# Gated layers as 2x2 block products with seven multiplications

## Chip, cores and metric

One core of a Trainium2 chip runs the whole program. The metric is the device time of one execution in microseconds, median of the runs shown.

## What is computed

Two transformer blocks over 512 tokens of 1024 features, in fp32, one sequence. The second block has two layers, and each of these has two gated layers with the attentions between them:

```python
def swiglu(h, w_gate, w_up, w_down):
    return (jax.nn.silu(h @ w_gate) * (h @ w_up)) @ w_down
...
    for l in range(DEPTH_2):
        x = x + 0.5 * swiglu(rmsnorm_2(x, ffn1_norm[l]), ffn1_w_gate[l], ffn1_w_up[l], ffn1_w_down[l])
        x = x + token_mixing(rmsnorm_2(x, mix_norm[l]), positions, w_in[l], ...)
        x = x + 0.5 * swiglu(rmsnorm_2(x, ffn2_norm[l]), ffn2_w_gate[l], ffn2_w_up[l], ffn2_w_down[l])
    return rmsnorm_2(x, final_norm)
```

The inner width D_FF is 2816, 22 tiles of 128 features.

## The kernel before

Activations lie with features on the 128 partitions and the 512 tokens along the free axis, so a matrix of 1024 features is eight row tiles of 128x512. TensorE works in its fast fp32 form, and to keep the accuracy each operand is split into a high part (ScalarE copies it into that form) and a low part (the rest, which VectorE or GpSimd subtracts). A product of two tiles is then three TensorE products: high by high, high by low, low by high (`mm3`, lines 227 to 229).

```python
    def split(self, hi, lo, src, pool=False):
        self.nc.scalar.activation(hi, src, AF.Copy)
        (self.nc.gpsimd if pool else self.nc.vector).tensor_tensor(lo, src, hi.bitcast(F32), op=ALU.subtract)
```

These are lines 202 and 203; most splits of the kernel are recorded under them. Weights come from HBM in units of 128x1024 (512 KB) through SyncE's queue into `wraw` and are split into `whi` and `wlo`; there are three buffers of each.

`ffn` is a gated layer; it runs four times (`which` 0 to 3). For each of the 22 inner tiles it loads a unit of gate and one of up, does 24 products of 512 columns for each into a PSUM bank, multiplies both by the norm's factor `rb` (lines 885 and 887, VectorE), takes silu (886, ScalarE), the product of the two (888, VectorE), and splits the result into `hid`. Since a norm's factor belongs to a token, that is, to a column, it can be applied behind the product: the operands `xs` are x times the gain, already split when x was finished, and `rb` itself is made by a chain of small steps (`norm`) whose TensorE pieces are put between the first products of the layer. Then come eight output tiles, each 66 products over all 22 tiles of `hid` (units of 8, 8 and 6 tiles). `residual` (line 852) adds half the result to x, and splits and squares it for the next norm (lines 206, 207, 324, 325). In the last gated layer the last output tile is done in two halves of the tokens, so that the final norm of one half lies beside the products of the other.

TensorE takes the instructions of the first two tiles of a layer in the order written; otherwise, in the gated layers, a planner with modelled durations orders each engine's instructions. Every engine then takes its own in that order. The attention (`mix`, lines 999 on) is written out in order for TensorE. Operands of layers lie in 28 slots of 4 KB for each partition, taken in turn.

## Time and profile before

| | us |
|---|---|
| median of 3 runs | 3024.08 |
| lowest and highest run | 3020.95, 3024.65 |
| span of the profiled execution | 3020.9 |
| granted TensorE clock in it, mean | 0.991 of 2.4 GHz |
| four gate/up stages | 253, 248, 248, 247 |
| four down stages | 123, 122, 122, 125 |
| two attention stages | 323, 324 |

The span runs from the first to the last instruction of the profiled execution. Stages are bounded by the first product of each kind, to a microsecond. What is left is the first block, 873 us, and the end.

### The profile page before, as it was taken

Reading aid. Unit: us, or ns where it says so; the run is one execution under the profiler, and the core shown is the slowest. Engines: PE = TensorE matmul, PEld = TensorE weight load, DVE = VectorE, ACT = ScalarE, POOL = GpSimd, SP = SyncE. Lnnn points to the kernel's source line nnn. Section 1 sums busy time; section 2 is a strip of 40 time slices with the busy share of each in tenths; the row PEclk is TensorE's granted clock in tenths of the full one; section 3 lists DMA queues with packets and bytes.
Section 4 is the critical chain, followed back from the end, with each engine's and each line's share of the span. In section 5 each row is a group of like instructions: output and inputs, shape, how many; then the busy total and the mean of one; then the engine's idle time right before and its main releaser. Section 6 shows DMA issues by size and latency. Waiting matters only on the chain.

```text
span 3020.9 us, 35009 instructions
## 1 busy us (share of the span) xinstructions
PE 2935.9 (97%) x13845; PEld 2387.9 (79%) x13845; DVE 1601.3 (53%) x2388; ACT 1272.8 (42%) x1917; POOL 417.8 (14%) x255
## 2 busy tenths in 40 slices
PE   6999999999999999989999999999999889999998
PEld 5888978888878888876788888888888767888887
DVE  7765665524455443488764443344433887644433
ACT  5665454423333222376743322223223767532322
POOL 4233430000000000243400000000002434100000
PEclk9999999999999999999999999999999999999999
DMA  6334332222223223211022223232322110122222
GB/s 233 111 123 140 137 135 82 92 97 94 95 92 100 92 94 96 89 56 43 29 70 93 96 89 96 94 98 91 96 89 94 57 49 29 63 91 98 92 95 73
DMA packets 79544, 278.06 MB, mean 92 GB/s; under 512 B 8811, under 2 KB 11115, under 8 KB 79380
## 3 DMA queue, kind: packets, MB, share of 16 engines
q1 hardware_dynamic: 79380, 275.82, 28.0%
q8 instruction: 109, 1.79, 0.2%
q14 instruction: 55, 0.45, 0.0%
HBM read 273.69 MB, written 2.10 MB: 91 GB/s over the span
## 4 chain that ended last, share of the span: by engine, by line
PE 89%; DVE 6%; issue 2%; ACT 1%; POOL 1%; DMA 0%; SPq 0%; POOLq 0%; DVEq 0%; ACTq 0%
PE up L227 5%; PE up L229 5%; PE up L228 5%; PE down L228 5%; PE gate L227 5%; PE down L229 5%; PE down L227 5%; PE gate L228 5%; PE gate L229 5%; PE ff L227 4%; PE ff L229 4%; PE ff L228 4%; PE pv L1320 2%; PE ptr L1302 2%; PE wo L229 1%
## 5 line engine op out<-in xcount | busy, mean ns | idle before, releaser
L202 ACT ACTIVATE whi<-wraw 128x1024 fp32r<-128x1024 f32 (+2 forms) x472 | 490.3, 1039 | 1286.9 <-issue 503.1
L203 DVE TENSOR_TENSOR wlo<-wraw,whi 128x1024 fp32r<-128x1024 f32 (+1 forms) x406 | 502.9, 1239 | 428.3 <-ACT whi L202 426.0
L203 POOL TENSOR_TENSOR wlo<-wraw,whi 128x1024 fp32r<-128x1024 f32 (+1 forms) x66 | 155.6, 2361 | 914.8 <-ACT whi L202 903.9
L228 PE MATMUL down<-hid,whi 128*128 128x512 f32 (+1 forms) x726 | 281.6, 388 | 0.0
L229 PE MATMUL down<-hid,wlo 128*128 128x512 f32 (+1 forms) x726 | 281.5, 388 | 0.0
L227 PE MATMUL down<-hid,whi 128*128 128x512 f32 (+1 forms) x726 | 280.9, 387 | 0.0
L887 DVE TENSOR_TENSOR u<-up,rb 128x512 f32<-128x512 f32 x88 | 60.8, 691 | 282.0 <-PE up L229 281.9
L227 PE MATMUL up<-xs,whi 128*128 128x512 f32 x528 | 209.4, 397 | 0.0
L227 PE MATMUL gate<-xs,whi 128*128 128x512 f32 x528 | 208.9, 396 | 0.0
L228 PE MATMUL up<-xs,whi 128*128 128x512 f32 x528 | 208.6, 395 | 0.0
L228 PE MATMUL gate<-xs,whi 128*128 128x512 f32 x528 | 208.5, 395 | 0.0
L229 PE MATMUL up<-xs,wlo 128*128 128x512 f32 x528 | 208.5, 395 | 0.0
L229 PE MATMUL gate<-xs,wlo 128*128 128x512 f32 x528 | 207.8, 394 | 0.0
L272 POOL TENSOR_TENSOR y<-ms,mhalf 128x4 f32<-128x4 f32 (+2 forms) x24 | 27.1, 1128 | 1293.2 <-DVE ms L271 1290.2
L885 DVE TENSOR_TENSOR t<-gate,rb 128x512 f32<-128x512 f32 x88 | 60.8, 691 | 197.5 <-PE gate L229 189.3
L228 PEld LDWEIGHTS down<-hid,whi 128*128 128x128 f32 x726 | 136.4, 188 | 30.7
L227 PEld LDWEIGHTS down<-hid,whi 128*128 128x128 f32 x726 | 136.3, 188 | 30.7
L229 PEld LDWEIGHTS down<-hid,wlo 128*128 128x128 f32 x726 | 136.5, 188 | 29.4
L227 PEld LDWEIGHTS up<-xs,whi 128*128 128x128 f32 x528 | 99.2, 188 | 24.2
L229 PEld LDWEIGHTS up<-xs,wlo 128*128 128x128 f32 x528 | 99.3, 188 | 23.8
L229 PEld LDWEIGHTS gate<-xs,wlo 128*128 128x128 f32 x528 | 99.2, 188 | 23.8
L227 PEld LDWEIGHTS gate<-xs,whi 128*128 128x128 f32 x528 | 99.2, 188 | 23.6
(562 smaller groups left out, 6844.0 us busy)
## 6 DMA issues: line engine op xcount, KB each, us to landing
wraw<-in_w2g SPq DMA_DIRECT2D x176, 512.0 KB, 3.5
wraw<-in_w2d SPq DMA_DIRECT2D x64, 512.0 KB, 3.5
ada<-in_ada SPq DMA_DIRECT2D x48, 512.0 KB, 5.3
wraw<-in_w1f SPq DMA_DIRECT2D x44, 512.0 KB, 3.5
wraw<-in_w1a SPq DMA_DIRECT2D x32, 512.0 KB, 3.4
wraw<-in_w1b SPq DMA_DIRECT2D x32, 512.0 KB, 3.4
wraw<-in_w2f SPq DMA_DIRECT2D x28, 512.0 KB, 3.5
wraw<-in_w2d SPq DMA_DIRECT2D x32, 384.0 KB, 3.0
```

Source lines behind the costliest of these rows:

```text
L202: self.nc.scalar.activation(hi, src, AF.Copy)
L203: (self.nc.gpsimd if pool else self.nc.vector).tensor_tensor(lo, src, hi.bitcast(F32), op=ALU.subtract)
L227: mm(out, ah, bh, start=start, stop=False)
L228: mm(out, ah, bl, start=False, stop=False)
L229: mm(out, al, bh, start=False, stop=stop)
L272: nc.gpsimd.tensor_tensor(y, ms, self.mhalf[:, :n], op=ALU.pow)
L885: nc.vector.tensor_tensor(t, og, rb, op=ALU.mult)
L887: nc.vector.tensor_tensor(u, ou, rb, op=ALU.mult)
L1302: nc.tensor.transpose(tr[:, b * P:(b + 1) * P], p[:, b * P:(b + 1) * P], self.c("ident"))
L1320: nc.tensor.matmul(o, values[b][:, h * P:(h + 1) * P], pt[i][:, b], start=b + i == 0, stop=b + i == NT)
```

## The change

A gated layer is cut into 2x2 blocks. For gate and up, the two rows of the weights' block matrix are gate (a11, a12) and up (a21, a22) of one inner tile, its columns the first and the last four of the eight row tiles of x; the other factor's blocks are these halves of x by the first and the last 256 tokens (b11, b12, b21, b22). For down, the rows are two neighbouring output tiles (n1 and n2), and the columns the two halves of a chunk of inner tiles. The 22 inner tiles make four chunks: three of 3 + 3 tiles, one of 2 + 2. A block product takes seven products of blocks where the plain way takes eight:

- sums of weights: s1 = a21 - a22, s3 = a21 - a11, s2 = a11 - s1, s4 = a12 - s2 (`g_block_weights`), each made on the chip and split like the three blocks that are used as they are;
- sums of the other factor: t1 = b12 - b11, t3 = b22 - b12, t2 = b22 - t1, t4 = b21 - t2 (`sums_of`), also made and split on the chip;
- seven products of 256 columns into three banks (`block`): into bank e one after the other a11 b11, s2 t2, s1 t1, s4 b22, into g s3 t3 and a22 t4, into f a12 b21. Between two of them the bank is read (`on`), so its running sums go to the right quarter of the result. The last product of a block is put off behind the second product of the next one.

The sums join tokens whose norm factors differ, so the factor cannot come in behind the products; the block operands of gate and up are made from x times gain times `rb` once the norm is there (`operands`); the first two inner tiles (0 and 3) stay plain products of `xs` (`Plain`, as before). A down product of a chunk begins when the first gate/up block of the next chunk is issued, and its seven results are added to x at once, each 256 columns (`Down.on`). After the last chunk `finished` does for two output tiles what `residual` did. The last unit of the last layer stays plain, in two halves of the tokens (`End`).

The six instructions marked `True` or `nc.gpsimd` in `g_block_weights` run on GpSimd, and in `operands` the sums of two of the four row pairs. Weights of an item are prepared one item ahead, one step after each product (`between`), and loaded two ahead. For the first gated layer the product of x with the earlier block's final norm moves from the chain of that norm into `operands`. TensorE now takes the instructions of a whole gated layer in the order written. `whi` and `wlo` of all stages come from one pool of ten buffers, `wraw` has four, the sums of weights two; slots go from 28 to 25. The last load of weights is now named for each load, so that loads stay in order. The host lays out up before gate, and the down weights by chunk (`_blocks`). A scratch area for descriptors shrinks to 256.

The core of the diff (comments dropped from other functions are left out):

```diff
-WBUFS = (3, 3, 3)
-SLOTS = 28
+WBUFS = (4, 2, 10)
+SLOTS = 25
+CHUNKS = [([0, 1, 2], [3, 4, 5]), ([6, 7, 8], [9, 10, 11]), ([12, 13, 14], [15, 16, 17]), ([18, 19], [20, 21])]
+H = T // 2
...
-        raw = self.wp.tile([P, 1024], F32, name="wraw", tag="wraw", bufs=WBUFS[2])
-        self.last_load = self.nc.sync.dma_start(out=raw[:, :f], in_=src[:, :f])
+        raw = self.wp.tile([P, 1024], F32, name="wraw", tag="wraw", bufs=WBUFS[0])
+        with self.tc.issue_after(self.last_load.ins) if self.last_load else ExitStack():
+            self.last_load = self.nc.sync.dma_start(out=raw[:, :f], in_=src[:, :f])
         return raw
     def split_weights(self, raw, nk, n, pool=False):
         f = nk * n
-        lo = self.wp.tile([P, 1024], F32R, name="wlo", tag="wlo", bufs=WBUFS[0])
-        hi = self.wp.tile([P, 1024], F32R, name="whi", tag="whi", bufs=WBUFS[1])
+        lo, hi = self.kilo("wlo"), self.kilo("whi")
         self.split(hi[:, :f], lo[:, :f], raw[:, :f], pool)
         return (hi[:, :f].rearrange("p (k n) -> p k n", k=nk), lo[:, :f].rearrange("p (k n) -> p k n", k=nk))
+    def kilo(self, name, dt=F32R):
+        return self.wp.tile([P, 1024], dt, name=name, tag="w1k", bufs=WBUFS[2])
     def weights(self, src, nk, n, pool=False):
         return self.split_weights(self.load_weights(src, nk * n), nk, n, pool)
...
-            rb = yield from self.g_bcast4(r, "rbx")
-            for n in range(KT):
-                yield 1.0
-                nc.vector.scalar_tensor_tensor(x[:, n], x[:, n], self.par("final1", n), rb, op0=ALU.mult, op1=ALU.mult)
+            box.rbx = yield from self.g_bcast4(r, "rbx")
...
+    def sums_of(self, up, down, half, pool):
+        nc = self.nc
+        v = nc.gpsimd if pool else nc.vector
+        th, tl, b = self.slot("th")[:, :1024], self.slot("tl")[:, :1024], self.slot("bs")[:, :1024]
+        u1, u2, d1, d2 = up[:, :H], up[:, H:], down[:, :H], down[:, H:]
+        ta, tb = self.tmp("ta"), self.tmp("tb")
+        t1, t3, t2, t4 = ta[:, :H], ta[:, H:], tb[:, :H], tb[:, H:]
+        nc.scalar.activation(b[:, :H], u1, AF.Copy)
+        v.tensor_tensor(t1, u2, u1, op=ALU.subtract)
+        v.tensor_tensor(t3, d2, u2, op=ALU.add)
+        nc.scalar.activation(b[:, H:3 * H], down, AF.Copy)
+        v.tensor_tensor(t2, d2, t1, op=ALU.add)
+        v.tensor_tensor(t4, d1, t2, op=ALU.subtract)
+        nc.vector.tensor_tensor(b[:, 3 * H:], u1, b[:, :H].bitcast(F32), op=ALU.subtract)
+        nc.vector.tensor_tensor(half, down, b[:, H:3 * H].bitcast(F32), op=ALU.subtract)
+        for i, t in enumerate((ta, tb)):
+            self.split(th[:, i * T:(i + 1) * T], tl[:, i * T:(i + 1) * T], t, pool)
+        out = {n: (th[:, i * H:(i + 1) * H], tl[:, i * H:(i + 1) * H]) for i, n in enumerate(("t1", "t3", "t2", "t4"))}
+        out["b11"] = b[:, :H], b[:, 3 * H:]
+        out["b21"] = b[:, H:2 * H], half[:, :H]
+        out["b22"] = b[:, 2 * H:3 * H], half[:, H:]
+        return out
...
+    def g_block_weights(self, raw, kh):
+        nc, n = self.nc, kh * P
+        (a21, a22), (a11, a12) = ((r[:, :n], r[:, n:2 * n]) for r in raw)
+        s13, s24 = (self.wp.tile([P, 1024], F32, name=name, tag="ws", bufs=WBUFS[1]) for name in ("s13", "s24"))
+        s1, s3, s2, s4 = s13[:, :n], s13[:, n:2 * n], s24[:, :n], s24[:, n:2 * n]
+        w = {}
+        def two(name, src, pool):
+            t = self.kilo(name)
+            hi, lo = t[:, :n], t[:, n:2 * n]
+            self.split(hi, lo, src, pool)
+            w[name] = tuple(x.rearrange("p (k n) -> p k n", k=kh) for x in (hi, lo))
+        two("a11", a11, False)
+        nc.vector.tensor_tensor(s3, a21, a11, op=ALU.subtract)
+        nc.vector.tensor_tensor(s1, a21, a22, op=ALU.subtract)
+        yield
+        nc.gpsimd.tensor_tensor(s2, a11, s1, op=ALU.subtract)
+        two("s3", s3, True)
+        yield
+        two("s2", s2, True)
+        yield
+        nc.gpsimd.tensor_tensor(s4, a12, s2, op=ALU.subtract)
+        two("a12", a12, False)
+        yield
+        two("a22", a22, False)
+        yield
+        two("s1", s1, True)
+        yield
+        two("s4", s4, True)
+        yield
+        return w
+    def block(self, w, acts, on, between):
+        def product(out, a, b, first):
+            wh, wl = w[a]
+            n = len(acts)
+            for k in range(n):
+                xh, xl = acts[k][b]
+                self.mm3(out, wh[:, k], wl[:, k], xh, xl, first and k == 0, k == n - 1, skip_group_check=True)
+                self.spend(3 * H * CYCLE)
+            between()
+        e = self.bank("g", "e")[:, :H]
+        product(e, "a11", "b11", True)
+        on("e1", e)
+        g = self.bank("s", "g")[:, :H]
+        product(g, "s3", "t3", True)
+        on("g1", g)
+        self.close_block()
+        product(e, "s2", "t2", False)
+        on("e2", e)
+        f = self.bank("v", "f")[:, :H]
+        product(f, "a12", "b21", True)
+        on("f", f)
+        product(g, "a22", "t4", False)
+        on("g2", g)
+        product(e, "s1", "t1", False)
+        on("e3", e)
+        def last():
+            product(e, "s4", "b22", False)
+            on("e4", e)
+        between = lambda: None
+        self.open_block = last
...
     def ffn(self, xs, norm, which, gain):
-        nc, a = self.nc, self.a
-        hid = self.act_slots("hid", NF2)
+        nc, a, x = self.nc, self.a, self.x
         order = ExitStack()
         order.enter_context(self.in_order("ffn"))
-        for i in range(NF2):
-            if i == 2:
-                order.close()
-            og, ou = self.bank("g", "gate"), self.bank("g", "up")
-            self.gemm_fm(og, self.weights(a["w2g"][which, i, 0], KT, P), xs)
-            self.gemm_fm(ou, self.weights(a["w2g"][which, i, 1], KT, P), xs)
-            while norm.rb is None:
-                norm.step()
-            rb = norm.rb
-            t, u = self.tmp("t"), self.tmp("u")
-            nc.vector.tensor_tensor(t, og, rb, op=ALU.mult)
-            nc.scalar.activation(t, t, AF.Silu)
-            nc.vector.tensor_tensor(u, ou, rb, op=ALU.mult)
-            nc.vector.tensor_tensor(t, t, u, op=ALU.mult)
-            self.split(hid[i][0], hid[i][1], t)
-        nx = self.act_slots("xs", KT) if gain else None
+        acts = []
+        def operands():
+            while norm.rb is None or which == 0 and norm.rbx is None:
+                yield 0.3
+            gains = norm.gain if which == 0 else self.par(("ffn1n0", "ffn2n0", "ffn1n1", "ffn2n1")[which], 0, KT)
+            half = self.halves("xhalf", 4)
+            for k in range(4):
+                t = [self.tmp("xr"), self.tmp("xr")]
+                for i in range(2):
+                    kk = k + 4 * i
+                    nc.vector.scalar_tensor_tensor(t[i], x[:, kk], gains[:, kk:kk + 1], norm.rb, op0=ALU.mult, op1=ALU.mult)
+                    if which == 0:
+                        nc.vector.scalar_tensor_tensor(x[:, kk], x[:, kk], self.par("final1", kk), norm.rbx, op0=ALU.mult, op1=ALU.mult)
+                acts.append(self.sums_of(*t, next(half), k % 2 == 1))
+                yield 0.5
+        operands = Chain(self, operands())
...
+                pairs.append((c, hidden.pop(k1[j]), hidden.pop(k2[j])))
+                if c < len(CHUNKS) - 1:
+                    combine()
+        def combine():
+            while pairs:
+                c, h1, h2 = pairs.pop(0)
+                hid[c].append(self.sums_of(h1, h2, next(half), False))
+                if not gain and c == len(CHUNKS) - 1:
+                    s = self.tmp("b12", F32R)
+                    nc.scalar.activation(s[:, :H], h1[:, H:], AF.Copy)
+                    nc.vector.tensor_tensor(s[:, H:], h1[:, H:], s[:, :H].bitcast(F32), op=ALU.subtract)
+                    hid[c][-1]["b12"] = s[:, :H], s[:, H:]
...
+                og, ou = self.bank("g", "gate"), self.bank("g", "up")
+                for n, (o, u) in enumerate(((og, w[1]), (ou, w[0]))):
+                    for k, _ in enumerate(self.g_gemm(o, u, xs)):
+                        if k % 3 == 2:
+                            between()
+                while norm.rb is None:
+                    norm.step()
+                t, u = self.tmp("t"), self.tmp("u")
+                nc.vector.tensor_tensor(t, og, norm.rb, op=ALU.mult)
+                nc.scalar.activation(t, t, AF.Silu)
+                nc.vector.tensor_tensor(u, ou, norm.rb, op=ALU.mult)
+                nc.vector.tensor_tensor(t, t, u, op=ALU.mult)
+                keep(me.i, t)
...
+                def on(what, o):
+                    if what == "e1":
+                        nc.scalar.activation(t[:, :H], o, AF.Copy)
+                    elif what == "g1":
+                        nc.scalar.activation(u[:, H:], o, AF.Copy)
+                    elif what == "e2":
+                        nc.scalar.activation(u[:, :H], o, AF.Copy)
+                    elif what == "f":
+                        nc.vector.tensor_tensor(t[:, :H], o, t[:, :H], op=ALU.add)
+                        nc.scalar.activation(t[:, :H], t[:, :H], AF.Silu)
+                    elif what == "g2":
+                        nc.vector.tensor_tensor(u[:, :H], o, u[:, :H], op=ALU.add)
+                    elif what == "e3":
+                        nc.vector.tensor_tensor(u[:, H:], o, u[:, H:], op=ALU.add)
+                    else:
+                        nc.scalar.activation(t[:, H:], o, AF.Silu)
+                        nc.vector.tensor_tensor(t, t, u, op=ALU.mult)
+                        keep(me.i, t)
+                self.block(w, acts, on, between)
...
+        def finished(n):
+            if gain:
+                if n == 0:
+                    nx[:] = self.act_slots("xs", KT)
+                self.split_scaled(nx[n][0], nx[n][1], x[:, n], self.par(gain, n))
+            self.sq_acc(acc, x[:, n], n == 0)
             if not gain:
-                nc.scalar.activation(self.x[:, n], self.x[:, n], AF.Copy, scale=self.par("final2", n))
+                nc.scalar.activation(x[:, n], x[:, n], AF.Copy, scale=self.par("final2", n))
...
+                where = {"e1": (n1, left), "g1": (n2, right), "e2": (n2, left), "f": (n1, left), "g2": (n2, left),
+                         "e3": (n2, right), "e4": (n1, right)}
+                def on(what, o):
+                    n, cols = where[what]
+                    nc.vector.scalar_tensor_tensor(x[:, n, cols], o, 0.5, x[:, n, cols], op0=ALU.mult, op1=ALU.add)
+                    if what == "e4" and me.c == len(CHUNKS) - 1:
+                        finished(n1)
+                        finished(n2)
+                self.block(w, hid[me.c], on, between)
+                combine()
...
+        first = CHUNKS[0]
+        plain = [first[0][0], first[1][0]]
+        ups = [[Up(i) for j in range(len(k1)) for i in (k1[j], k2[j]) if i not in plain] for k1, k2 in CHUNKS]
+        downs = [[Down(c, m) for m in range(4)] for c in range(len(CHUNKS))]
+        if not gain:
+            downs[-1][-1] = End(len(CHUNKS) - 1, 3)
+        items = [Plain(i) for i in plain] + ups[0]
+        for c in range(1, len(CHUNKS) - 1):
+            items += ups[c][:1] + downs[c - 1] + ups[c][1:]
+        items += ups[-1] + downs[-2] + downs[-1]
+        raws = [items[0].load(), items[1].load()]
+        w = drain(items[0].prepare(raws[0]))
+        for n, item in enumerate(items):
+            if n + 2 < len(items):
+                raws.append(items[n + 2].load())
+            ahead, done = (items[n + 1].prepare(raws[n + 1]) if n + 1 < len(items) else iter(())), []
+            def between():
+                if not done:
+                    try:
+                        next(ahead)
+                    except StopIteration as e:
+                        done.append(e.value)
+            item.run(w, between)
...
```

## Rows read from the trace of the kernel before

**Rows 1.** The page: span, busy time, and two groups of the costliest.

```profile
span 3020.9 us, 35009 instructions
PE 2935.9 (97%) x13845; PEld 2387.9 (79%) x13845; DVE 1601.3 (53%) x2388; ACT 1272.8 (42%) x1917; POOL 417.8 (14%) x255
...
L887 DVE TENSOR_TENSOR u<-up,rb 128x512 f32<-128x512 f32 x88 | 60.8, 691 | 282.0 <-PE up L229 281.9
...
L885 DVE TENSOR_TENSOR t<-gate,rb 128x512 f32<-128x512 f32 x88 | 60.8, 691 | 197.5 <-PE gate L229 189.3
```

**Rows 2.** Windows by stage: a gated layer's two, an attention, a gated layer's two.

```profile
core 0: us, PE busy (x) PEld busy (x) DVE busy (x) ACT busy (x) POOL busy (x), PEclk, DMA share, GB/s
873.00:1126.00 253.00, 251.52 (x1084) 202.17 (x1083) 126.28 (x188) 79.17 (x98) 2.01 (x2) 0.99 0.29 94
1126.00:1249.00 123.00, 123.00 (x532) 99.55 (x531) 39.77 (x46) 33.47 (x40) 4.79 (x2) 1.00 0.29 91
1249.00:1572.00 323.00, 301.73 (x1618) 243.67 (x1617) 242.14 (x454) 214.01 (x410) 114.78 (x67) 0.97 0.17 53
1572.00:1820.00 248.00, 248.00 (x1071) 199.96 (x1070) 112.82 (x142) 74.59 (x92) 1.02 (x1) 1.00 0.29 93
1820.00:1942.00 122.00, 122.00 (x527) 98.64 (x526) 41.88 (x47) 32.67 (x39) 0.00 (x0) 1.00 0.30 93
```

**Rows 3.** Timeline of TensorE, down products: start, us, engine and line.

```profile
1199.64 0.39 PE L229 MATMUL down<-hid,wlo 128*128 128x512 f32 x1
...
1205.94 0.39 PE L229 MATMUL down<-hid,wlo 128*128 128x512 f32 x1
```

**Rows 4.** Timeline of TensorE, products of 256 columns, first and 41st.

```profile
338.33 0.28 PE L227 MATMUL gva<-whi,xn 128*128 128x256 f32 x1
...
342.99 0.28 PE L227 MATMUL gva<-whi,xn 128*128 128x256 f32 x1
```

**Rows 5.** Timeline of GpSimd and of VectorE, 367.4 to 383 us.

```profile
367.46 11.84 POOL L740 TENSOR_TENSOR gv<-gv,lng 128x1024 f32<-128x1024 f32 x4 [1.78 <-ACT whi L202]
...
373.61 3.42 DVE L203 TENSOR_TENSOR wlo<-wraw,whi 128x1024 fp32r<-128x1024 f32 x1
376.95 3.43 DVE L743 TENSOR_TENSOR gv<-gv,lnb 128x1024 f32<-128x1024 f32 x1
380.31 2.29 DVE L203 TENSOR_TENSOR wlo<-wraw,whi 128x1024 fp32r<-128x1024 f32 x1
```

**Rows 6.** By line and tile: count, duration ns min/median/max, first and last start.

```profile
L203 DVE TENSOR_TENSOR wlo<-wraw,whi x406: 957/1225/3424, 60.2 to 2991.2; 128x1024 fp32r<-128x1024 f32 x120, 128x768 fp32r<-128x768 f32 x16
L203 DVE TENSOR_TENSOR hid<-t,hid x88: 682/685/694, 894.4 to 2886.3; 128x512 fp32r<-128x512 f32 x88
L203 DVE TENSOR_TENSOR mvl<-mva,mvh x8: 417/420/425, 102.1 to 301.4; 128x256 fp32r<-128x256 f32 x8
L1312 DVE TENSOR_TENSOR ptl<-ptr,pth x128: 671/681/692, 1304.0 to 2595.7; 128x512 fp32r<-128x512 f32 x128
L207 DVE SCALAR_TENSOR_TENSOR xs<-x,par,xs x40: 742/746/2359, 1143.1 to 2638.6; 128x512 fp32r<-128x512 f32 x40
L325 DVE TENSOR_TENSOR acc<-acc,sq x69: 677/684/693, 7.2 to 2992.1; 128x512 f32<-128x512 f32 x69
L203 POOL TENSOR_TENSOR wlo<-wraw,whi x66: 1533/2404/2763, 17.1 to 2574.4; 128x1024 fp32r<-128x1024 f32 x58, 128x640 fp32r<-128x640 f32 x8
L203 POOL TENSOR_TENSOR qq<-qbf,qq x16: 1272/1292/1317, 1451.5 to 2576.8; 128x512 fp32r<-128x512 f32 x16
L947 POOL TENSOR_TENSOR x<-x,rb x6: 727/730/739, 3004.8 to 3015.9; 128x256 f32<-128x256 f32 x6
L202 ACT ACTIVATE hid<-t x88: 614/633/638, 893.8 to 2885.6; 128x512 fp32r<-128x512 f32 x88
L689 ACT ACTIVATE gv<-gva x8: 364/380/386, 328.8 to 357.2; 128x256 f32<-128x256 f32 x8
```

**Rows 7.** Timeline of GpSimd, two instructions in a row.

```profile
195.99 4.76 POOL L426 TENSOR_TENSOR ada<-ada,cb 128x1024 f32<-128x1024 f32 x2
```

**Rows 8.** The chain that ended last, longest pieces: start, us, what.

```profile
373.69 3.34 DVE wlo L203
377.03 2.37 DVE gv L743
...
1250.36 2.37 DVE xs L207
```

**Rows 9.** Timeline of GpSimd in the attention.

```profile
1448.81 2.63 POOL L203 TENSOR_TENSOR kk<-kbf,kk 64x512 fp32r<-64x512 f32 x2 [2.49 <-ACT kk L202]
1451.53 1.28 POOL L203 TENSOR_TENSOR qq<-qbf,qq 128x512 fp32r<-128x512 f32 x1
1452.77 2.39 POOL L203 TENSOR_TENSOR wlo<-wraw,whi 128x1024 fp32r<-128x1024 f32 x1
```

**Rows 10.** Timeline of TensorE, ScalarE and VectorE, start of the second gated layer.

```profile
1571.71 0.39 PE L227 MATMUL gate<-xs,whi 128*128 128x512 f32 x1
...
1583.27 0.60 ACT L308 ACTIVATE rb<-bc_b 128x512 f32<-128x512 f32 x1 [4.02 <-PE bc_b L301]
...
1583.90 0.69 DVE L885 TENSOR_TENSOR t<-gate,rb 128x512 f32<-128x512 f32 x1 [2.73 <-ACT rb L308]
```

More of the change, by code (lines that the diff above doesn't have):

```diff
@@ L1 @@
+import functools
 import math
@@ new lines, in halves @@
+    def halves(self, name, n):
+        for i in range((n + 1) // 2):
+            s = self.slot(f"{name}{i}")
+            for j in range(2):
+                yield s[:, j * T:(j + 1) * T]
+    def g_block_weights(self, raw, kh):
[28 more added lines that the diff above has]
+        return w
```

141 lines of the change are left out of this document (103 added, 38 removed).

## Prediction

> **What bounds the kernel now.** I read the page's busy shares first: TensorE is busy for 97% of the span, VectorE for 53%, GpSimd for 14%, and VectorE's largest waits in the gated layers are for TensorE's last product of a tile [rows 1]. The table by stage says where: in the four gated layers TensorE is busy all the time, and GpSimd, which does 114.8 us in an attention stage, does 0 to 5 us in one of these [rows 2]. Their stages take 253 + 123 + 248 + 122 + 248 + 122 + 247 + 125 = 1488 us, half of the kernel. Since records of products overlap, I price a product by the distance of starts: 27 steps of 512 columns from 1199.64 to 1205.94, 0.2333 us each [rows 3]; 40 of 256 columns from 338.33 to 342.99, 0.1165 us each [rows 4]. Half the columns cost half the time, although each product loads its own weights, so small products carry no penalty.
>
> **TensorE's part of the change.** A gate/up pair was 48 products of 512 columns, 11.20 us; as a block (7 products x 4 tiles x 3 parts = 84 of 256 columns) it is 9.79. A pair of output tiles of one chunk was 36 products (8.40 us) and becomes 63 of 256 columns (7.34); in the last chunk 24 (5.60) and 42 (4.89). A layer has 20 blocks of the first kind, 12 and 4 of the others, and two plain pairs: it saves 28.2 + 12.7 + 2.8 = 43.7 us, four layers 175. If TensorE stayed the bound, the span of 3020.9 would become 2846.
>
> **What the blocks cost elsewhere.** Each block's weights are now added up on the chip (s1 to s4) and split seven times. Six of these instructions go to GpSimd (s2, s4, and the low parts of s1 to s4), 512 wide in a gate/up block, 384 or 256 in a down block. Five go to VectorE (s1, s3, three low parts). All of them read two operands in SBUF. So do the product t*u, and eight instructions for a pair of hidden tiles, which make its sums and low parts (five of 256, three of 512).
>
> Can VectorE and GpSimd do this side by side? From 367.46 us GpSimd runs four 1024-wide products of two SBUF operands, its queue without a pause, and VectorE's 1024-wide instructions of two SBUF operands beside them last 3.42 and 3.43 us [rows 5]. The same kind takes 1.225 us in the median, and its longest record is 3.42 us; a VectorE instruction that reads PSUM is never stretched (671 to 692 ns over 128, many of them under GpSimd's work) [rows 6]. The stretched ones start 3.34 and 3.36 us apart [rows 5]. GpSimd alone does two such in 4.76 us, 2.38 each [rows 7]. So the two take turns: a turn of 3.35 us costs 0.97 us more than GpSimd's own for VectorE's 1024 elements, 0.95 ns an element. The chain of waits goes through such instructions already, among them 2.37 us in the first split after a gated layer, which is 746 ns in the median [rows 6, 8].
>
> The Trainium skill has the same lock in "SBUF — State Buffer", section "Who interferes with whom": a VectorE instruction with two SBUF inputs and a GpSimd instruction that reads SBUF shut each other out for the whole instruction. Whole instructions would make that turn 1.225 + 2.40 = 3.6 us, where the rows show 3.35; a time by the rule is rival 3.
>
> *A gate/up block.* GpSimd's 512-wide split is recorded with 1.29 us [rows 6], and where its splits wait for ScalarE in between, three starts come in 1452.77 - 1448.81 us, 1.32 each [rows 9]: 6 x 1.32 = 7.92. VectorE: six of 512 (s1, s3, three low parts, t*u) are 3072 elements, and half of a pair's 2816 are 1408: 4480 x 0.95 ns = 4.26. Together 12.18 us against 11.20 before and the 9.79 that TensorE now needs: +0.98 a block, +19.6 a layer. Bounds: GpSimd without waits at 1.25 (two records of 2.40 [rows 6] overlap by 0.04 [rows 7]) gives 11.76; whole instructions added (6 x 0.69, and half of 5 x 0.42 + 3 x 0.69) give 14.15. I stay near the lower one, since it has the size of the turns in rows 5.
>
> *A down block of three tiles.* GpSimd takes 0.73 us for 256 and 1.29 for 512 [rows 6], so 1.01 for 384, with the same 0.03 behind it 1.04; six are 6.24. VectorE: 5 x 384 x 0.95 = 1.82. Together 8.06 against 8.40: -0.34, twelve are -4.1 (bounds 7.64 and 9.0).
>
> *A down block of the last chunk* also finishes two tiles of x: a split (746 ns) and a sum of squares (684 ns) each, both of two SBUF operands [rows 6]. 6 x 0.76 + (5 x 256 + 4 x 512) x 0.95 = 7.72 us against 5.60: +2.12, four are +8.5 (bounds 7.3 and 9.5).
>
> *The start of a layer.* Before, products started on x without the norm, which came in behind them. Operands of a block need the norm first. It is used 12.2 us into a layer (1583.90 against 1571.7) [rows 10], and the two plain pairs cover TensorE until 22.4. In the 10.2 us between stand: eight x*rb of 512 (3.9), two sums on VectorE (2 x 2816 x 0.95 = 5.4) and its share of the other two (1.5), these on GpSimd (2 x (4 x 0.76 + 2 x 1.32) = 11.4), and 2.0 of the plain pairs: 24.2, so TensorE waits 14 us. Bounds: 8 if GpSimd's last sums come in behind the first products; 26 if the first block's weights (12.2) stand before them.
>
> *At no cost:* DMA (1 MB a block in 12 us is 86 GB/s, these stages move 93 now [rows 2]); ScalarE (seven splits of 0.63, five short ones of 0.38, two and a half of a pair's [rows 6]: under 8 of 12 us); VectorE's readings of PSUM (0.42 each [rows 6], outside the lock, under GpSimd's time); SP's loads, which keep their order. If VectorE's readings lost that cover, 3 x 0.42 would join a gate/up block, 1.3 us. The smaller slot count (25 for 28) and the common pool of weights touch the attention, whose instructions stay: 0, at most 10 us a stage.
>
> **Sum.** A layer: 19.6 - 4.1 + 8.5 + 14 = +38.0; four: +152. The last layer makes no next operands and ends with a plain unit: -5; the first also applies the norm of the block before to x, eight more of 512: +4. Span 3021 + 151 = 3172. The median of the runs stands 3.2 us above this span: 3175.
>
> **Rivals.**
> 1. *TensorE stays the bound.* VectorE's instructions fall into GpSimd's waits for ScalarE and hardly ever take a turn. This decides once no more than 3.3 us of a block's 4.26 collide (11.20 - 7.92). With a block at 9.79, the start (14) and a last chunk at VectorE's own 8 us an item, a layer saves 43.7 - 14 - 12.4 = 17 us: 2955; with those two hidden as well 2850. For it: low parts wait for ScalarE, so GpSimd has pauses. Against it: the two engines together want 12.2 us, and TensorE takes their weights in a strict order.
> 2. *The queues couple.* VectorE takes its instructions in order, and a reading of PSUM for which TensorE waits (a block adds several products into one bank, and each must be read before the next) stands behind one that is locked out for 1.3 us. Such a reading has two products' time, 2.8 us in a gate/up block, 2.1 and 1.4 in a down block. At 1 us lost in each of 4 x 36 blocks: 144 more, 3320. For it: the waits of rows 5; against it: a block has three banks, the next one others.
> 3. *Whole instructions shut each other out.* A block at 14.15, down blocks at 9.0 and 9.5, the start at 20: +102 a layer, 3430. Against it: turns of 3.35 us. The Trainium skill's rule above is this one, and these turns differ from it by 0.27 us in 3.6.
> 4. *Even.* Fixed parts of all instructions overlap: a gate/up block at 11.1, down blocks at 7.34 and 7.7, the start at 10: +4 a layer, 3040; with the start hidden too, no change.
>
> **Chances and range.** The forecast (3050 to 3260) 0.56, rival 2 0.18, rival 3 0.05, rival 1 0.16, rival 4 0.05. About 0.2%, 6 us, can be told from no change here. Rival 1 is faster, part of rival 4 the same: faster 0.17, same 0.03, slower 0.80. The range leaves out rival 1 and the far ends of rivals 2 and 3: 3000 to 3370. It takes in the lower bounds of all terms (11.2 - 9.1 + 6.8 + 8 a layer: 3092); all the upper ones at once are rival 3.
>
> **What would show it.** TensorE idle between its products, released by GpSimd's low parts; a gate/up block every 12.2 us, a down block every 8.1; VectorE's two-operand instructions of 512 in these stages with a mean over 1 us, where they take 0.69 now; GpSimd busy for over 60% of them; a hole of some 14 us, 22 us into a layer. The prediction is wrong if those instructions keep 0.69 us beside a busy GpSimd, if blocks come every 9.8 us, or if TensorE waits for readings of PSUM and not for weights.

## The result, and the profile after

The changed kernel takes 3266.01 us (median of four runs, 3261.74 to 3271.91) against 3022.51 (3020.46 to 3024.65): a ratio of 1.0806, 95% interval 1.0791 to 1.0822. It is slower, as forecast (3175, range 3000 to 3370), by 243 us where the forecast said 151. The profiled execution has a span of 3261.4 us and a mean granted clock of 0.952 (before 0.991).

The page of the changed kernel, span and busy time, answers to [rows 1]:

```profile
span 3261.4 us, 48352 instructions
...
PE 2910.5 (89%) x18249; PEld 2590.6 (79%) x18249; DVE 2487.9 (76%) x3720; ACT 1699.4 (52%) x3143; POOL 1622.2 (50%) x1161
```

TensorE has lost 8 points of its share, VectorE has won 23 and GpSimd 36. Windows of the first gated layer, the first attention and the second gated layer, to be read beside [rows 2] (same columns):

```profile
878.40:1312.08 433.68, 365.75 (x2706) 351.56 (x2704) 377.54 (x551) 213.06 (x435) 300.25 (x228) 0.92 0.25 76
1312.08:1650.65 338.57, 313.77 (x1640) 253.55 (x1639) 256.21 (x470) 219.88 (x417) 126.14 (x72) 0.94 0.19 58
1650.65:2071.86 421.21, 360.11 (x2730) 346.48 (x2729) 370.72 (x517) 212.03 (x434) 297.67 (x227) 0.94 0.26 81
```

From a layer's first product to the next stage the four gated layers now take 433.7, 421.2, 418.5 and 432.9 us (the third from the end of the second's last block, before which 16 of its products have already run, the last to the end of the span), where they took 375.4, 370.5, 370.2 and 384.5: +206. The attentions went from 323 and 324 to 338.6 and 338.2: +30. The first block is 5 us longer. Together 241, the difference of the spans.

Groups of VectorE's and of GpSimd's instructions in the second gated layer (busy us, mean ns of one, idle before them and its releaser):

```profile
L208 DVE TENSOR_TENSOR a<-wraw,a 128x512 fp32r<-128x512 f32 x60 | 75.3, 1255 | 7.9 <-ACT a L207 7.9
...
L1135 DVE SCALAR_TENSOR_TENSOR x<-e,x 128x256 f32<-128x256 f32 x63 | 24.8, 411 | 2.1 <-PE e L237 1.9
L929 DVE TENSOR_TENSOR s<-wraw 128x512 f32<-128x512 f32 x19 | 22.9, 1205 | 5.9 <-POOL s L208 5.9
L1099 DVE TENSOR_TENSOR t<-t,u 128x512 f32<-128x512 f32 x20 | 22.5, 1125 | 12.2 <-ACT t L1098 12.2
...
L208 POOL TENSOR_TENSOR s<-s,s 128x512 fp32r<-128x512 f32 x80 | 122.9, 1548 | 39.9 <-ACT s L207 29.4 <-PE g L237 10.4
```

Of VectorE's 512-wide instructions with both operands in SBUF, which took 0.69 us [rows 6], the low parts of weights, the first weight sum (L929) and t*u (L1099) are stretched to 1.1 to 1.3 us on average; others that meet GpSimd less often are stretched less (the second weight sum, L930, to 0.88). GpSimd's low parts go from 1.29 to 1.55. VectorE's readings of PSUM, 256 wide and 0.41 us long, are not stretched. Who lets TensorE wait in the same layer (us in total, times, longest):

```profile
PE e L235 <- DVE u L1096: 32.1, 14, 3.5
PE up L235 <- DVE t L1063: 15.5, 1, 15.5
PE e L235 <- DVE x L1135: 10.7, 15, 3.9
```

All three are VectorE's readings of a PSUM bank. No wait of TensorE in this layer ends with a low part from GpSimd. One of them in the timeline (GpSimd, VectorE, TensorE; in brackets the idle time before and what ended it):

```profile
1837.13 1.59 POOL L932 TENSOR_TENSOR s<-wraw,s 128x512 f32<-128x512 f32 x1 [2.22 <-issue]
1838.68 1.72 POOL L208 TENSOR_TENSOR s<-s,s 128x512 fp32r<-128x512 f32 x1
...
1836.32 0.68 DVE L930 TENSOR_TENSOR s<-wraw 128x512 f32<-128x512 f32 x1
1836.92 0.68 DVE L208 TENSOR_TENSOR tl<-tb,th 128x512 fp32r<-128x512 f32 x1
1837.53 1.74 DVE L208 TENSOR_TENSOR a<-wraw,a 128x512 fp32r<-128x512 f32 x1
1839.19 0.41 DVE L1096 TENSOR_TENSOR u<-e,u 128x256 f32<-128x256 f32 x1
...
1839.66 0.46 PE L235 MATMUL e<-bs,s 128*128 128x256 f32 x1 [3.48 <-DVE u L1096]
```

A low part of weights starts on VectorE 0.4 us after GpSimd's s2 and ends 0.55 us after that is done. Behind it in VectorE's queue stands the reading of bank e, and TensorE, which wants to put the block's last product into that bank, has waited 3.48 us. About 1 us of this is the stretch of the low part; in the rest VectorE does a sum of the next block's weights, a low part of hidden sums, the low part's own 0.7 us and the reading. Work for later blocks holds up the block that is running.

### The profile page after: what moved, and what is told of

Same layout as the page of the kernel before. It is cut to its first block, busy times and chain, and to the rows that moved or that the text cites. A ratio compares the mean times of both kernels' runs of the same rounds, so it can differ in the third digit from the quotient of the medians.

```text
span 3261.4 us, 48352 instructions
## 1 busy us (share of the span) xinstructions
PE 2910.5 (89%) x18249; PEld 2590.6 (79%) x18249; DVE 2487.9 (76%) x3720; ACT 1699.4 (52%) x3143; POOL 1622.2 (50%) x1161
## 5 line engine op out<-in xcount | busy, mean ns | idle before, releaser
L208 POOL TENSOR_TENSOR s<-s,s 128x512 fp32r<-128x512 f32 (+2 forms) x572 | 780.1, 1372 | 276.8 <-ACT s L207 217.1
L208 DVE TENSOR_TENSOR a<-wraw,a 128x512 fp32r<-128x512 f32 (+2 forms) x429 | 482.9, 1126 | 44.9 <-ACT a L207 43.3
L207 ACT ACTIVATE s<-s 128x512 fp32r<-128x512 f32 (+2 forms) x572 | 324.6, 570 | 342.9 <-POOL s L932 88.4
L932 POOL TENSOR_TENSOR s<-wraw,s 128x512 f32<-128x512 f32 (+2 forms) x143 | 175.0, 1224 | 566.0 <-DMA wraw<-in_w2g 390.2
L208 DVE TENSOR_TENSOR wlo<-wraw,whi 128x1024 fp32r<-128x1024 f32 (+1 forms) x152 | 202.5, 1333 | 161.2 <-ACT whi L207 156.2
L235 PE MATMUL e<-th,s 128*128 128x256 f32 x988 | 293.2, 297 | 18.1 <-DVE x L1135 9.3
L235 PE MATMUL e<-bs,s 128*128 128x256 f32 x494 | 161.6, 327 | 160.5 <-DVE u L1096 128.4
L236 PE MATMUL e<-tl,s 128*128 128x256 f32 x988 | 291.2, 295 | 0.0
L237 PE MATMUL e<-th,s 128*128 128x256 f32 x988 | 290.6, 294 | 0.0
L235 PEld LDWEIGHTS e<-th,s 128*128 128x128 f32 x988 | 201.6, 204 | 21.1 <-ACT t L1085 9.6
L237 PEld LDWEIGHTS e<-th,s 128*128 128x128 f32 x988 | 200.5, 203 | 0.0
L937 POOL TENSOR_TENSOR s<-wraw,s 128x512 f32<-128x512 f32 (+2 forms) x143 | 195.8, 1369 | 1.5
L929 DVE TENSOR_TENSOR s<-wraw 128x512 f32<-128x512 f32 (+2 forms) x143 | 135.5, 947 | 38.0 <-POOL s L208 30.7
L237 PE MATMUL e<-bs,s 128*128 128x256 f32 x494 | 150.3, 304 | 0.0
L236 PE MATMUL e<-bs,a 128*128 128x256 f32 x494 | 139.1, 282 | 8.1 <-DVE bs L897 8.1
L235 PE MATMUL e<-bs,a 128*128 128x256 f32 x494 | 139.1, 282 | 5.0 <-ACT bs L891 5.0
```

What stands on the lines that cost most here:

```text
L235: mm(out, ah, bh, start=start, stop=False)
L236: mm(out, ah, bl, start=False, stop=False)
L237: mm(out, al, bh, start=False, stop=stop)
L929: nc.vector.tensor_tensor(s3, a21, a11, op=ALU.subtract)
L932: nc.gpsimd.tensor_tensor(s2, a11, s1, op=ALU.subtract)
L937: nc.gpsimd.tensor_tensor(s4, a12, s2, op=ALU.subtract)
```

## Experiments

Times are compared with the kernel before on the same chip (3024.26 for the first four, 3023.84 for the next four, 3023.19 for the three after them). Each of the first six kernels was run once, so a few us between them mean nothing. "A block every n us" is the mean distance of the first f product of neighbouring blocks of one kind.

**Is it GpSimd's help?** All six instructions of `g_block_weights` that GpSimd did go to VectorE.

```diff
-        nc.gpsimd.tensor_tensor(s2, a11, s1, op=ALU.subtract)
-        two("s3", s3, True)
+        nc.vector.tensor_tensor(s2, a11, s1, op=ALU.subtract)
+        two("s3", s3, False)
```

(and so for the other four)

> All eleven instructions of a block's weights on VectorE, none on GpSimd. Turns: VectorE's own work of a gated layer is about 285 us when nothing stretches it, and the six instructions add 20 x 6 x 0.685 + 12 x 6 x 0.55 + 4 x 6 x 0.41 = 131, so 416 a layer against 415 to 434 now: the time stays within 50 us of 3266, 512-wide splits come out at 0.68 us each, and GpSimd's help is shown to be worth nothing. Rival, two engines that work side by side and a layer set by TensorE's waits for readings of PSUM: 131 us more in VectorE's queue come on top, over 3600.

3058.38 us: 208 less than the change, although VectorE has 858 instructions more. Gate/up blocks come every 10.0 to 10.3 us (change: 12.1 to 12.6), down blocks of three tiles every 7.9 (8.75). VectorE's 512-wide instructions are recorded with 0.70 us and start only 0.60 apart when its queue is full, which is why it manages more than the sum by records said; the expectation (within 50 us of 3266) was missed by 158 us. Two helpers are slower here than one. The spans show where the rest of the change's cost lies: the four gated layers together are 7 us below the kernel before, while the attentions take 341.0 and 343.5 us for its 323 and 324.

**Is it GpSimd's slowness or the lock?** In the first of two kernels the low parts of s1 to s4 are left out, and their high parts stand in for them; in the second GpSimd makes three fills of the low part in place of it, so GpSimd is as busy and the products still use what it writes, but these four of its six instructions read nothing. The sums s2 and s4 stay on GpSimd and still read, and the fills, unlike the low parts, need not wait for ScalarE's high part.

```diff
-            self.split(hi, lo, src, pool)
+            nc.scalar.activation(hi, src, AF.Copy)
+            for _ in range(3):
+                nc.gpsimd.memset(lo.bitcast(F32), 0.0)
```

(second kernel, for the four with `pool`; the first has `lo = hi` in place of the loop)

> Leaves out the low parts of s1 to s4 (the high parts stand in their place), so GpSimd keeps two of six instructions a block, and VectorE and TensorE keep all of theirs. Turns: VectorE is stretched by two instructions and not by six, its 285 us a layer fall below TensorE's 325 plus the start; a layer of 345 to 365, in all 2960 to 3040, a gate/up block every 9.8 to 10.3 us. Rival, readings of PSUM: VectorE's queue is as long as before, 3220 to 3270.

> As the run without GpSimd's low parts, but in the place of each low part GpSimd writes zeros there three times, which reads nothing. If GpSimd's reading is what shuts VectorE out, the time is that of the run without low parts, within 30 us, and VectorE's 512-wide instructions keep 0.68 us beside the writes. If any GpSimd work does it, blocks come at 11 to 12 us and the time is above 3150.

3045.45 us (5 above the expected range) and 3041.74 (within 30 us of the first, as expected), with the same blocks: every 10.3 to 10.5 us and 7.6 to 7.7. Of the second kernel, a window within the second gated layer, three groups of that layer and a piece of its timeline:

```profile
1600.00:1900.00 300.00, 279.54 (x2264) 273.58 (x2263) 225.29 (x396) 177.16 (x363) 246.38 (x417) 0.98 0.29 93
...
L208 DVE TENSOR_TENSOR a<-wraw,a 128x512 fp32r<-128x512 f32 x60 | 53.4, 889 | 33.0 <-ACT a L207 16.9 <-POOL s L928 15.9
L934 DVE TENSOR_TENSOR s<-wraw 128x512 f32<-128x512 f32 x20 | 13.8, 689 | 6.2 <-POOL s L928 2.4 <-ACT s L926 2.1 <-DMA wraw<-in_w2g 1.5
...
L928 POOL MEMSET s<- 128x512 f32 x240 | 119.9, 526 | 36.6 <-PE e L237 20.1 <-PE wo L237 7.2 <-PE up L237 4.9
...
1749.50 3.33 POOL L928 MEMSET s<- 128x512 f32 x6 [1.11 <-PE e L237]
1753.05 1.62 POOL L937 TENSOR_TENSOR s<-wraw,s 128x512 f32<-128x512 f32 x1 [0.22 <-ACT a L207]
...
1755.09 1.30 POOL L942 TENSOR_TENSOR s<-wraw,s 128x512 f32<-128x512 f32 x1
...
1751.63 0.68 DVE L934 TENSOR_TENSOR s<-wraw 128x512 f32<-128x512 f32 x1
1752.23 0.68 DVE L935 TENSOR_TENSOR s<-wraw 128x512 f32<-128x512 f32 x1
...
1753.77 1.45 DVE L208 TENSOR_TENSOR tl<-tb,th 128x512 fp32r<-128x512 f32 x1
1755.14 1.80 DVE L208 TENSOR_TENSOR a<-wraw,a 128x512 fp32r<-128x512 f32 x1
```

GpSimd is busy for 246 of 300 us, more than in the change (228 of 300, from 1700 us on), yet VectorE's weight sums beside its fills (L934, L935) keep their 0.69. Two low parts soon after them meet GpSimd's s2 and s4, which read, and last 1.45 and 1.80 us. The low parts of weights are of both kinds: the layer's 60 have a mean of 889 ns, and the 39 of the window's 58 that meet neither s2 nor s4 last 689 on average. TensorE's waits for VectorE's readings of bank e fall from 42.8 us in the second layer to 7.3. So neither GpSimd's load nor the wait for its results costs the time, but its reading. The Trainium skill, "SBUF — State Buffer", section "Who interferes with whom", has both halves of this: a VectorE instruction with two SBUF inputs contends with a GpSimd instruction that reads SBUF, not with one that only writes it. The runs agree: the first weight sum takes 1205 ns where GpSimd reads and 689 where it fills.

**Which blocks cost it?** The gate/up blocks alone, with plain down products for each chunk; and the down blocks alone, with every gate/up pair plain.

```diff
-                return self.g_block_weights(raw, me.kh)
+                out = []
+                for r in raw:
+                    out.append(self.split_weights(r, 2 * me.kh, P))
+                    yield
+                return out
...
-        plain = [first[0][0], first[1][0]]
-        ups = [[Up(i) for j in range(len(k1)) for i in (k1[j], k2[j]) if i not in plain] for k1, k2 in CHUNKS]
+        plain = []
+        ups = [[Plain(i) for j in range(len(k1)) for i in (k1[j], k2[j]) if i not in plain] for k1, k2 in CHUNKS]
```

(above the dots the first kernel, where `Down.run` does products of 512 columns as before; below them the second)

> Gate and up as blocks as in the change, down as plain products of each chunk, with hidden tiles split as before. Turns: a gate/up block needs 6 x 1.32 + (6 + 1) x 512 x 0.95 ns = 11.3 us, a layer 22 + 20 + 20 x 11.3 + 123 = 391, in all about 3160. Rival, readings of PSUM: gate/up blocks stay at 12.2 us, a layer 409, 3230.

> Gate and up as plain products throughout, down as blocks as in the change: no operands at the start, no wait for the norm. Turns by the prediction's terms: twelve down blocks at 8.1 and four at 7.7 us, 128 a layer against 123 before, in all 3040. By the blocks measured in the change (8.75 and 5.7): 128 as well, 3040, and an end of the layer that is late by VectorE's backlog, 5 to 15 us in each of three layers, so 3055 to 3085. If the down blocks gained what TensorE saves there, 108 a layer: 2965.

3113.31 (+89) and 3061.65 us (+38). A gate/up block, now without sums of hidden tiles, comes every 11.26 us in the first layer and 11.1 in the others (11.3 expected). The last three layers take 383 to 400 us where 391 was expected; the total expected from this, 3160, was 47 us too high. In the second kernel, whose time is within its expected 3055 to 3085, down blocks come every 7.78 us within the first two chunks, but one in each layer takes 13 to 14.5. The parts sum to +127, the whole is +243: together they cost more. That this is because they share VectorE's queue is my reading; only the whole has sums of hidden tiles beside gate/up blocks.

**The slots.** One edit of the kernel before.

```diff
-SLOTS = 28
+SLOTS = 25
```

> The kernel before with 25 slots and not 28. If the slots are what makes each attention stage 15 us longer in the change, its stages come at 338 us here and the time at 3050; if it is the late end of the gated layer ahead of it, the stages stay at 323 and 324 and the time within 6 us of the kernel before.

3020.75 us, with attentions of 323 and 321 us: the slots alone do not make the attention's 15 us. The common pool of weights was not tried by itself.

**A version without the lock and with fewer sums.** Gate/up blocks all on VectorE, the sums of operands too, three plain pairs ahead, down plain; to the edits of the first kernel and of the gate/up one come these.

```diff
-                acts.append(self.sums_of(*t, next(half), k % 2 == 1))
+                acts.append(self.sums_of(*t, next(half), False))
...
-        plain = [first[0][0], first[1][0]]
+        plain = [first[0][0], first[1][0], first[0][1]]
```

> Blocks for gate and up alone, all eleven instructions of a block's weights and all operand sums on VectorE, three plain pairs at the start of a layer and not two, down plain. No turns: a gate/up block at 9.9 to 10.0 us. The operands are ready about 12 + 20 + 8 us into a layer, the three pairs cover 33.6: a wait of 6 to 12 us. A layer 33.6 + 9 + 19 x 9.95 + 123 = 355 against 370: 2940 to 2985, faster than both kernels. If VectorE alone cannot keep up (its queue held 10.04 us in a block with the down blocks beside it), 3000 or more.

3016.61 us (9 runs), a ratio of 0.9975 (0.9965 to 0.9984): below the kernel before. Gate/up blocks come every 9.9 us, TensorE's own time but for 0.1, so VectorE keeps up alone. The second layer takes 358.5 us where it took 370.5, although its first block begins only 47 us into it (33.6 are covered by plain pairs). The expectation (2940 to 2985) was missed all the same, by 32 us: the attentions still take 334.4 and 335.2 us, 22 more than before, and the first and the last layer take 373 and 378 us where 355 was expected.

**Two low parts on GpSimd, every third pair plain.** Blocks and plain pairs take turns, so that GpSimd's work meets less of VectorE's.

```diff
-        two("s3", s3, False)
+        two("s3", s3, True)
...
+        kind = (Up, Even, Up, Up, Even, Up)
```

(against the version before; s1 likewise. The operands' sums of two of the four row pairs go back to GpSimd too, each row pair gets one more split for the plain pairs, the pool has nine buffers, and there are 26 slots.)

> As the run before, but of the low parts of a block's weights two go to GpSimd, and a third of the remaining gate/up pairs are plain, made from the block operands: each plain pair gives VectorE and GpSimd time to catch up. 13 blocks at 10 us, 6 pairs at 11.2: 33.6 + 9 + 130 + 67 + 123 = 363 a layer, 2970 to 3010. If turns with GpSimd cost as in the change, blocks are longer by about 0.5 us each: up to 3030.

3050.91 us, 1.0093 (1.0078 to 1.0109). It is 0.9% slower, and above both expectations (2970 to 3010, at most 3030): TensorE waits longer for the readings of the plain tiles at a layer's start (25.6 us in two waits in the second layer, 8.9 in one in the version before). Which of the edits makes them longer was not separated.

**The start and the attention.** Two edits of the all-VectorE version, alone and together: the steps of `operands` spread out, and the low parts of the attention's first four weight units moved from GpSimd to VectorE.

```diff
                 acts.append(self.sums_of(*t, next(half), False))
-                yield 0.5
+                yield 5.0
...
-            return lambda: [self.weights(src[i], 4, 256, True) for i in range(2)], run
+            return lambda: [self.weights(src[i], 4, 256, name != "vd") for i in range(2)], run
```

(the queries and keys dq0 and dk0 likewise)

> The kernel of the all-VectorE gate/up blocks (3016.6 us), with the four steps that make a layer's block operands set 5 us of products apart where they stood 0.5 us apart. Theory: the wait at a layer's start there is one of order in VectorE's queue: the plain tiles' readings of PSUM stand behind all operand sums, so TensorE waits some 10 us for a bank (38.9 us in 4 waits for the reading of the gate tile) and the first block begins 47 to 60 us into a layer where the plain tiles could cover until 33.6. Spread out, the readings come on time, the first block begins 36 to 40 us into a layer, and four layers save 8 to 12 us each: 2970 to 2985. Rival: the operand sums themselves (4 steps of about 4.7 us on VectorE, and 4.6 us of weights' low parts beside them, from 12 us on) end no earlier, since VectorE is full in that stretch: then only the place of the wait moves, from a bank to the first block, and the time stays at 3012 to 3020.

> The same kernel (3016.6 us), operands as they were, with the low parts of the attention's first four weight units (the first values, and the first queries and keys of the differential heads) on VectorE where GpSimd made them. Theory: the attention stages lose 11 us against the kernel before because all eight output tiles of a gated layer now end within its last 24 us, so VectorE still has several splits and sums of squares to do when GpSimd splits the attention's first weights; these 1024-wide instructions lock VectorE's (2.4 to 2.9 us where 0.7 is usual), and TensorE waits 8 us within the first 10 us of the stage. On VectorE they cost 1.2 us each and lock nothing: 3 to 6 us less a stage, two stages: 3004 to 3011. Rival: VectorE is late by its own work at the end of the layer and gets 4.8 us more of it here: no change, 3014 to 3020.

> Both edits together. If both theories hold the savings add: 2960 to 2978. If both rivals hold: 3010 to 3020. If only the first holds, 2970 to 2985 again.

Spread alone: 3019.0 us, 0.9987 (0.9978 to 0.9995), no gain, and nothing of the 8 to 12 us a layer that were expected; the rival was right. Windows at the start of the second layer, of the version with spread steps and of the one without:

```profile
1607.00:1627.00 20.00, 16.73 (x66) 13.19 (x65) 20.00 (x39) 10.17 (x20) 0.00 (x0) 0.91 0.15 53
1627.00:1647.00 20.00, 17.18 (x122) 16.31 (x121) 17.10 (x32) 10.76 (x23) 0.00 (x0) 0.91 0.16 54
```

```profile
1605.00:1625.00 20.00, 11.22 (x42) 9.06 (x43) 20.00 (x41) 11.09 (x20) 0.00 (x0) 0.83 0.09 32
1625.00:1645.00 20.00, 20.00 (x142) 18.62 (x142) 16.81 (x29) 10.79 (x22) 0.00 (x0) 1.00 0.22 75
```

VectorE is busy for all of the first 20 us in both. Part of TensorE's wait moves from the first window into the second; the layer takes 359.1 us for 358.5.

The attention's weights alone: 3006.28 us, 0.9942 (0.9930 to 0.9955). The time is within the expected 3004 to 3011, so the theory holds; the saving, 10 us, is near the upper end of what was expected. At the start of the first attention without the edit (GpSimd, VectorE, TensorE):

```profile
1249.10 5.46 POOL L208 TENSOR_TENSOR wlo<-wraw,whi 128x1024 fp32r<-128x1024 f32 x2 [3.46 <-ACT whi L207]
...
1249.73 2.62 DVE L212 SCALAR_TENSOR_TENSOR xs<-x,par,xs 128x512 fp32r<-128x512 f32 x1 [0.19 <-ACT xs L211]
1252.28 2.83 DVE L333 TENSOR_TENSOR acc<-acc,sq 128x512 f32<-128x512 f32 x1
1255.03 0.68 DVE L1119 SCALAR_TENSOR_TENSOR x<-down,x 128x512 f32<-128x512 f32 x1
...
1256.52 0.58 PE L235 MATMUL vda<-whi,xs 128*128 128x256 f32 x1 [3.72 <-ACT xs L211]
```

A split and a sum of squares take 5.3 us beside GpSimd's two splits, x waits behind them in the queue, and the attention's products wait for x. With the edit the stages take 326.1 and 329.9 us. Both edits together: 2998.47 us, 0.9925 (0.9911 to 0.9938), the fastest kernel here, 25 us below the one before. This misses all that was expected: no case had the second theory hold without the first. Its interval overlaps that of the attention edit alone (the runs are 2996.82 to 3002.98 for 3002.57 to 3006.63), so what the spread adds there is not settled.

**Does the kernel before gain by this edit too?** The same two lines of the attention in the kernel before:

```diff
-            return lambda: self.weights(a["w2f"][l, FM2_AT[key]], KT, P, pool=True), run
+            return lambda: self.weights(a["w2f"][l, FM2_AT[key]], KT, P, pool=key not in ("dq0", "dk0")), run
```

(and that of the values, as above)

> The kernel before, with the same edit of the attention's first weights alone (their low parts on VectorE). It tells whether the 10 us that this edit saved beside the gate/up blocks belong to them or to the kernel before as well. Theory: the kernel before finishes an output tile every 15.4 us, so only the last tile's split and sum of squares meet GpSimd's splits there; one split lasts 2.36 us where 0.75 is usual, so at most 2 us a stage are to be had: 3018 to 3024. Rival: the edit helps any kernel in the same way: 3010 to 3015.

3022.67 against 3022.76 us, 0.9999 (0.9990 to 1.0008). It does not (3018 to 3024 was expected). The cost belongs to what the new gated layers leave behind them; that it is their eight output tiles ending together in the last chunk is the theory that foresaw this, and it was not tried apart.

## Why the prediction came out as it did

**What held.** *The bound moves.* TensorE's products kept their price at the full clock, and VectorE and GpSimd set the pace by taking turns: from 1800 to 1900 us, in the second gated layer, GpSimd or a VectorE instruction with both operands in SBUF is on record for 96 of 100 us, TensorE for 90. Without the low parts on GpSimd the kernel is 208 to 224 us faster. *The price of a turn* (0.95 ns an element on top of GpSimd's time) gave 12.18 us for a gate/up block: measured means are 12.62, 12.24, 12.14 and 12.30 in the four layers, and 11.1 for 11.3 without the hidden tiles' sums. Rival 3 (whole instructions, 14.15 us a block) and rivals 1 and 4 (9.79 and 11.1) fall by these means. But hardly a block takes 12.2. In the second layer the distances run 12.5, 10.8, 14.9, 10.2, then 13.2, 13.6, 10.2, 15.2, 9.9 and so on. In the last three layers those in which VectorE does at least five of the eight instructions of a pair's hidden sums average 14.6, the others 10.9. The prediction gave each block half of these sums; by its own terms a block has 13.5 with all of them and 10.8 with none. The others fit, the full ones are 1.1 us longer than their turns. The other signs came too: stretched means over 1 us, GpSimd busy for 298 of 421 us (71%).

**What released TensorE was named wrongly.** The prediction let products wait for GpSimd's low parts, and said it would be wrong if they waited for readings of PSUM. They do: 42.8 us of the second layer's waits in blocks end so, none with a low part of GpSimd's and 0.4 with one of VectorE's. This is rival 2's release, but at a mean period near the forecast's and not at 1 us more for each block. That the time came within the range although this step was wrong is in part luck; as I read it, both ways of waiting follow the same load of the two engines. VectorE's queue holds readings, sums and low parts in one order, so its stretched work holds up the running block before late weights would hold up the next.

**Terms that were mis-sized** (four layers together came out at +206 for +151; the gate/up blocks have 12 of the 55, the first three points below 37, and blocks at the change from one kind to the other and the layers' ends the rest):

- *A down block of three tiles*: 8.75 us for 8.06. In each layer one of nine distances is 14.4 to 14.6, the other eight average 8.03. In that one the sums of the last chunk's hidden tiles stand ahead of the readings. The term was right, the exception was missing: +33 us in 48 blocks.
- *The start wait*: the first block begins 34.6, 42.2, 48.4 and 42.0 us into a layer, for 36.4 (22.4 + 14): +22 in all. In the first layer TensorE then waits 13.1 us more inside the first block, for its operands (bs, L891 and L897), which makes +35; VectorE there also applies the earlier block's norm (L1006), for which 4 us had been added. In the third layer TensorE waits 8.3 us for the sum of squares of x (L333) first. In the last three layers most of the hole does not come behind the two plain pairs but inside the second one:

```profile
1685.03 0.79 PE L235 MATMUL up<-xs,whi 128*128 128x512 f32 x1 [15.54 <-DVE t L1063]
...
1684.30 0.68 DVE L1063 TENSOR_TENSOR t<-gate,rb 128x512 f32<-128x512 f32 x1
```

The reading of the first plain tile (L1063) was issued behind the operands' sums. The run with spread steps shows what order is worth in the version with three plain pairs: little, since VectorE is full.

- *A block of the last chunk*: 5.2 to 5.8 us for 7.72, some -31 in 15 blocks (the last layer ends with a plain unit). The finishing of x was charged to the block but runs late, and comes out behind it: in the 48.4 us of the third layer's start, 6.2 more than the second's, and in the next term.
- *The attention at nothing* (at most 10 us a stage): +15.6 and +14.2. The reason given was slots and the common pool; the slots alone do not make it, the pool was not tried, and nearly all of it arises at a stage's start, from the late x and the last block's products that run on behind the boundary. The 12th product of `vdb` starts 10.1 us into the first stage of the kernel before and 23.9 into that of the change (second stage: 10.1 and 23.8). In the version with three plain pairs it starts at 20.0 (20.4), and with four low parts moved at 11.0 (14.1). The step that failed is "whose instructions stay": what stood before them did not. Some 4 us more arise in the middle of the first attention. In the version with three plain pairs TensorE waits there for a small step of a norm, 3.83 us (2.53 before), and the granted clock of the next 8 us is 0.51 (1.00 before). Why that step comes later was not tried.
- *The clock*, no term at all. After a wait TensorE, whose 256-wide products start 0.1165 us apart [rows 4], goes on like this (changed kernel):

```profile
936.54 0.58 PE L235 MATMUL e<-th,s 128*128 128x256 f32 x1 [3.91 <-ACT t L1085]
936.92 0.41 PE L236 MATMUL e<-tl,s 128*128 128x256 f32 x1
...
941.83 0.41 PE L235 MATMUL g<-th,a 128*128 128x256 f32 x1
942.04 0.32 PE L236 MATMUL g<-tl,a 128*128 128x256 f32 x1
```

24 steps from 936.92 to 942.04 are 0.213 us each. The granted clock of that stretch is 0.50, the 1.2 GHz level in place of 2.4 (columns as in [rows 2]):

```profile
936.92:942.04 5.12, 5.12 (x25) 5.12 (x25) 3.40 (x6) 3.18 (x5) 1.29 (x1) 0.50 0.62 209
```

Counting 256-wide products 0.19 to 0.235 us ahead of the next gives 219, 160, 151 and 186 in the four layers: an estimated 70 us more than at 0.1165, if each takes 0.213. The all-VectorE change has 162 of them, the version with three plain pairs 3. Some of this lies inside waits for VectorE that would have lasted until then anyway; how much of the 91 us between forecast and result it makes was not separated. It is contained in the block times above, so these do not give the turns' price alone.

## What to carry to other kernels

Fewer products pay only as far as the engines that feed and empty them have room: here 175 us of TensorE's time (by the prediction's prices) were traded for sums on two engines that cannot read side by side. Of the kernels tried here the trade paid (4 to 25 us) only in those with the gate/up sums on one engine and down products plain, and 10 of the 25 came from also moving the attention's first low parts; blocks for down together with that edit were not tried. When an engine is given new work, look at what stands behind it in its queue: readings of PSUM, and at a stage's end the results that the next stage starts on. Late ends and short waits had a second price here, in the products that followed at the lower clock.

## What the runs showed of the hardware that was not expected

- VectorE's records overlap: 512-wide fp32 instructions recorded with 0.68 to 0.70 us start 0.60 apart in a full queue, 256-wide ones of 0.41 start 0.33 apart. A load summed from records is 15% too high for the first and 24% for the second.
- GpSimd that only writes leaves VectorE's two-operand instructions beside it at 0.69 us, in a stretch where GpSimd is 82% busy; where it reads in the same run, they last up to 1.80.
- A wait of 3.91 us, behind several others, was followed by 5.12 us of products at a granted clock of 0.50.
